# The down projection of an FFN in one streaming-encoder kernel: its transfers in program order by need, its weights and first residuals each in the place of one old pool, its output tiles in a pool of their own

## The chip, the cores and the metric

The kernel runs on one core of a Trainium2 chip. The metric is device time of one execution in microseconds (us): the median of the timed runs. Of 3 runs of the kernel before it was 2545.82 us (2545.22 to 2546.44).

The engines have short names in the profile: PE is TensorE (its weight loads PEld), DVE is VectorE, ACT is ScalarE, POOL is GpSimd, and SP is SyncE, which in this kernel issues nearly all transfers (SPq is its queue).

## The reference

One layer of an encoder: attention with two groups of heads, an output projection, and then a gated FFN whose last product the change concerns.

```python
def trunk_layer(x, pos, chunk, past, lp, rel_bias, lam_init):
    ...
    mix = jnp.concatenate([o_d.reshape(B, L, D_DIFF), o_m.reshape(B, L, D_MLA)], axis=-1)
    x = x + mix @ lp['w_out']
    h = rmsnorm(x, lp['norm_ffn_g'])
    x = x + (jax.nn.silu(h @ lp['ffn_w_gate']) * (h @ lp['ffn_w_up'])) @ lp['ffn_w_down']
    return x, (kd, vd, ckv, krope)
```

The model dimension is 2048, the FFN dimension 5632. There are 576 tokens in all (64 of running streams, 512 new frames). A last RMSNorm with `final_norm_g` follows. Everything is float32.

## The kernel before, in words

Operands are kept transposed, with features on the 128 partitions and the 576 tokens along the free axis, in two halves of 288. A float32 product is made of three matmuls in a faster format: each operand is split into a high part (a rounded copy, made by ScalarE) and a low part (the difference, made by VectorE), and high by high, high weight by low operand, and low weight by high operand are added up. The high and low parts of weights are called `wh` and `wl`, those of the tokens `bh` and `bl`.

The FFN's products go through one level of Winograd's form of Strassen's algorithm (`winograd`): a row of outputs needs seven products, numbered 1 to 7, instead of eight. A weight tile `raw` of 1 MB is loaded; products 1, 2 and 4 split parts of it directly, and the other four first form sums of parts, `ws`: those for products 5 and 7 on GpSimd, for 6 and 3 on VectorE. In the down projection the products come in the order 1, 5, 6, 2, 7, 3, 4 (`CHAIN`), and each has 12 matmuls of 288 columns, eight with `wh` (four operands `bh`, four `bl`) and then four with `wl`. A row has 84. `wh` and `wl` have two buffers each, `raw` has two, `ws` three.

Up and gate projection: 22 steps `u`, in each of which the tile `c` of gate outputs `g` is multiplied into that of the up outputs (GpSimd, `c<-c`, L1312), and the product is stored to HBM (`actspill`), with four sums of it for the later products (`sumspill`).

Down projection: the 22 steps are its contraction, in blocks of 4, 4, 4, 4, 4 and 2. A block has eight rows `d`; row `d` adds to the two residual tiles `y[2d]` and `y[2d+1]`, which are loaded from `x2spill` in the first block and stay in SBUF until the end. For a block, `builder` loads the operands as `bl` (from `actspill` or `sumspill`, 144 KB each), has ScalarE convert each to `bh` and VectorE subtract it. It is a generator: each `next` issues one conversion or one subtraction, and loads run `ahead` operands in front. `blX_S` is the operand of product X in slot S; slots 0 to 3 are used by one block and 4 to 7 by the next. For the first block the builder is advanced by `step` in the seven products of the last up projection, for the others by the products of the block before. The last block has no sums: `plain_rows` takes it in two halves of the tokens, and `finish` transposes the results, scales them on ScalarE or VectorE into output tiles `ot`, and stores them.

What sets the order of the work: TensorE's instructions are always issued as the program writes them. The others go through a scheduler that may move them, unless an instruction is pinned, with `pin` (from the start of the down projection on for the builder's instructions), or an `Engine` object has `ordered` set. In the down projection `pinned[0]` is set. SyncE's transfers are not pinned in the kernel before, so the scheduler puts them in an order of its own.

SBUF is handed out by pools that are stacked from the left (`fr`, `fw`, later `yp`) and from the right (`bc`, `rw`, `fb`, later `yy`). A tile in memory that an older pool held waits until the older tile has been used for the last time. `fb` holds the `c` tiles, `fw` the up projection's `wh`, `wl` and `ws`, `rw` the third buffer of `raw`. The kernel before opens `yy` (all 16 `y`) on the right in the place of `rw` and `fb`, and `yp` on the left in the place of `fw`. `yp` holds `wh`, `wl`, `ws` and also the output tiles `ot` and the small `vc` and `rc`, which is more than `fw` held, so that it reaches into `fb`'s place too.

All engines' operations that go through an `Engine` object carry line 125 in the profile; the matmuls are L1123 (with `wh`) and L1127 (with `wl`), GpSimd's `ws` L1092.

Of the kernel before, what the change touches and what calls it, by code (L numbers as in the profile page):

```python
# [11 lines left out]
F32 = mybir.dt.float32  # L12
# [7 lines left out]
P = 128  # L20
D = 2048
KC = D // P
# [5 lines left out]
TQ = NS + SEQ  # L28
# [103 lines left out]
def encoder_step(  # L132
# [19 lines left out]
    def load(dst, src):  # L152
        Q.dma_start(dst, src)

    def store(dst, src):
        Q.dma_start(dst, src)
# [1068 lines left out]
    def builder(m0, count, plain, ahead, by_product=False):  # L1225
# [21 lines left out]
        for n in range(ahead):  # L1247
            fetch(n)
        for n, (m, p) in enumerate(todo):
            fetch(n + ahead)  # L1250
            hi, lo = operands[m % 8, p]
            pin(S.activation(hi, f32(lo), AF.Copy))
            yield
            pin(V.tensor_tensor(lo, f32(lo), f32(hi), op=ALU.subtract))
            yield
# [16 lines left out]
    blocks = [4, 4, 4, 4, 4, 2]  # L1272

    turn = 0
# [80 lines left out]
    def down_rows(m0, n, d, slots, step):  # L1355
        raws = [load_raw(fr, w_down, m0 * 256, 2 * n, d * 256, 2)]
# [23 lines left out]
    def finish(h, ahead):  # L1380
# [27 lines left out]
        for i, (q, j) in enumerate(groups):  # L1408
            o, n = tok[h][j]
            ps = held.pop(0) if held else turned(q, j)  # L1410
            ot = yp.tile([P, 512], F32, name="ot", tag="ot", bufs=OT_BUFS)
# [9 lines left out]
            yield  # L1421

    pinned[0] = True
    first = 0
    for bi, n in enumerate(blocks):
        slots = [(first + k) % 8 for k in range(n)]
        if bi + 1 < len(blocks):
# [5 lines left out]
            for d in range(KC // 2):  # L1433
                if bi == 0:
                    for i in (2 * d, 2 * d + 1):
                        y.append(yy.tile([P, TQ], F32, name=f"y{i}"))
                        load(y[i], x2spill[i])
# [14 lines left out]
        first += n  # L1452
    close_yp()
    close_fr()
    close_yy()
    close_bc()
# [74 lines left out]
```

## Time and profile before

| | |
|---|---|
| median of 3 runs | 2545.82 us (2545.22 to 2546.44) |
| the profiled execution, its own time | 2543.0 us |
| its span | 2541.2 us |
| busy: PE, PEld | 96%, 94% of the span |
| busy: DVE, ACT, POOL | 71%, 44%, 29% |
| mean DMA | 121 GB/s |
| last matmul of the up projection starts | 1970.28 us |
| first matmul of the down projection starts | 1979.67 us |

Times in the profile are microseconds from the start of the span. A row of the timeline gives the start, the duration, engine, line, operation, output<-input, the number of instructions merged into it, and in brackets how long the engine had been idle before it and what released it. The duration of a merged row runs from its first start to its last end. In the table by windows the busy time of each engine stands with the count of its instructions; PEclk is TensorE's granted clock, 1.00 being full speed. A matmul's own time overlaps with the next one's, so the distance between starts is what counts.

### The profile page before, as it was taken

Reading aid. Unit: us, or ns where it says so; the run is one execution under the profiler, and the core shown is the slowest. Engines: PE = TensorE matmul, PEld = TensorE weight load, DVE = VectorE, ACT = ScalarE, POOL = GpSimd, SP = SyncE. Lnnn points to the kernel's source line nnn. Section 1 sums busy time; section 2 is a strip of 40 time slices with the busy share of each in tenths; the row PEclk is TensorE's granted clock in tenths of the full one; section 3 lists DMA queues with packets and bytes.
Section 4 is the critical chain, followed back from the end, with each engine's and each line's share of the span. In section 5 each row is a group of like instructions: output and inputs, shape, how many; then the busy total and the mean of one; then the engine's idle time right before and its main releaser. Section 6 shows DMA issues by size and latency. Waiting matters only on the chain. (4 is left out here: it accounts for less than half of the span.)

```text
span 2541.2 us, 44865 instructions
## 1 busy us (share of the span) xinstructions
PE 2446.1 (96%) x17847; PEld 2386.6 (94%) x17847; DVE 1799.2 (71%) x2826; ACT 1107.0 (44%) x2008; POOL 739.7 (29%) x614
## 2 busy tenths in 40 slices
PE   7999999989999999999999999999999899999997
PEld 6999999988999888999999999999999799999997
DVE  5555555556555567877777777777777899899975
ACT  5343334334343444444444444444445444444445
POOL 0000000000000164644545445454543222222236
PEclk9999999999999899999999999999999999999999
DMA  7533232334322453333333333333335642452334
GB/s 201 153 86 88 80 85 85 82 97 127 101 89 75 153 155 114 123 133 119 128 99 131 121 123 133 115 120 107 128 128 160 206 156 83 153 161 84 109 102 149
DMA packets 330563, 307.73 MB, mean 121 GB/s; under 512 B 24707, under 2 KB 298506, under 8 KB 330354
## 3 DMA queue, kind: packets, MB, share of 16 engines
q1 hardware_dynamic: 330354, 304.87, 38.3%
q8 instruction: 140, 2.29, 0.4%
q14 instruction: 69, 0.57, 0.1%
HBM read 250.82 MB, written 56.68 MB: 121 GB/s over the span
## 5 line engine op out<-in xcount | busy, mean ns | idle before, releaser
L1123 PE MATMUL m<-bh,wh 128*128 128x288 f32 x3584 | 968.9, 296 | 12.2 <-ACT wh L125 12.2
L1123 PE MATMUL m<-bl,wh 128*128 128x288 f32 x3584 | 968.3, 295 | 0.0
L1123 PEld LDWEIGHTS m<-bh,wh 128*128 128x128 f32 x3584 | 674.3, 188 | 13.2 <-ACT wh L125 13.2
L1123 PEld LDWEIGHTS m<-bl,wh 128*128 128x128 f32 x3584 | 678.1, 189 | 0.1
L1127 PE MATMUL m<-bh,wl 128*128 128x288 f32 x3584 | 585.4, 298 | 17.2 <-DVE wl L125 14.1
L1127 PEld LDWEIGHTS m<-bh,wl 128*128 128x128 f32 x3584 | 512.4, 189 | 30.1 <-DVE wl L125 29.7
L1092 POOL TENSOR_TENSOR ws<-raw 128x512 f32<-128x512 f32 x256 | 343.6, 1350 | 600.1 <-DVE wl L125 344.1
L125 ACT ACTIVATE wh<-ws 128x512 fp32r<-128x512 f32 (+1 forms) x340 | 288.8, 849 | 448.7 <-PE m L1123 293.3
L125 DVE TENSOR_TENSOR wl<-ws,wh 128x512 fp32r<-128x512 f32 (+1 forms) x340 | 379.5, 1116 | 113.7 <-ACT wh L125 113.3
L125 DVE TENSOR_TENSOR wl<-raw,wh 128x512 fp32r<-128x512 f32 x416 | 402.6, 981 | 27.6 <-ACT wh L125 17.4
L125 ACT ACTIVATE wh<-raw 128x512 fp32r<-128x512 f32 x416 | 249.7, 626 | 307.2 <-PE m L1123 274.6
L108 PE MATMUL ps<-xh,wh 128*128 128x296 f32 x960 | 220.8, 311 | 5.2 <-ACT xh L125 3.5
L108 PE MATMUL ps<-xl,wh 128*128 128x296 f32 x960 | 211.0, 301 | 0.9 <-DVE xl L125 0.9
L108 PE MATMUL ps<-xh,wl 128*128 128x296 f32 x960 | 210.8, 301 | 0.2 <-DVE wl L125 0.2
L108 PEld LDWEIGHTS ps<-xh,wh 128*128 128x128 f32 x960 | 157.1, 191 | 9.3 <-ACT xh L125 3.6
L108 PEld LDWEIGHTS ps<-xl,wh 128*128 128x128 f32 x960 | 157.4, 190 | 1.5 <-DVE xl L125 1.5
L108 PEld LDWEIGHTS ps<-xh,wl 128*128 128x128 f32 x960 | 157.2, 190 | 0.9 <-DVE wl L125 0.9
L125 DVE TENSOR_TENSOR y<-y,m 128x288 f32<-128x288 f32 x312 | 139.6, 447 | 25.8 <-PE m L1127 17.6
L125 DVE TENSOR_TENSOR ws<-ws,raw 128x512 f32<-128x512 f32 x128 | 92.3, 722 | 83.9 <-POOL ws L1092 77.5
L125 DVE TENSOR_TENSOR wl<-wr,wh 128x1024 fp32r<-128x1024 f32 (+1 forms) x110 | 117.6, 1070 | 35.3 <-ACT wh L125 33.9
L125 ACT ACTIVATE wh<-wr 128x1024 fp32r<-128x1024 f32 (+1 forms) x110 | 101.6, 928 | 74.1 <-PE ps L108 58.2
L1270 POOL TENSOR_TENSOR c<-c,rb 128x576 f32<-128x576 f32 x44 | 73.0, 1661 | 165.6 <-ACT c L125 165.6
(357 smaller groups left out, 3347.8 us busy)
## 6 DMA issues: line engine op xcount, KB each, us to landing
raw<-in_ffn_w_gate SPq DMA_DIRECT2D x44, 1024.0 KB, 7.0
raw<-in_ffn_w_up SPq DMA_DIRECT2D x44, 1024.0 KB, 5.3
raw<-in_ffn_w_down SPq DMA_DIRECT2D x40, 1024.0 KB, 5.4
wr<-in_w_in SPq DMA_DIRECT2D x60, 512.0 KB, 4.0
actspill<-c SPq DMA_DIRECT2D x44, 288.0 KB, 2.1
sumspill<-c SPq DMA_DIRECT2D x20, 576.0 KB, 3.0
bl<-sumspill SPq DMA_DIRECT2D x80, 144.0 KB, 3.8
bl<-actspill SPq DMA_DIRECT2D x68, 144.0 KB, 3.5
```

Source lines behind the costliest of these rows:

```text
L108: self.tc.keep_in_program_order(self.pe.matmul(out, lhsT, rhs, start=start, stop=stop))
L125: ins = issue(*args, **kwargs)
L1092: engine.tensor_tensor(w[:, k:k + m, :], pick(xs), pick(ys), op=op)
L1123: PE.matmul(banks[p], wh[:, k, :], x, start=first and new and k == 0 and x is hi, stop=False, skip_group_check=not new)
L1127: PE.matmul(banks[p], wl[:, k, :], hi, start=False, stop=last and k == n - 1, skip_group_check=not new)
L1270: G.tensor_tensor(g[:, f, :], g[:, f, :], rb2, op=ALU.mult)
```

## The change

The numerical work stays the same: no operation of the reference's arithmetic is added or dropped. Five things change.

1. SyncE's queue keeps the program's order from the start of the last up projection (`Q.ordered = True`) until the last block. What stands in the program where is then the order of the transfers.
2. The raw tile of `w_down` for a row is fetched two rows ahead (`fetch_raw`), no longer by `down_rows`. The builder of the first block issues its 28 loads product by product, in four at a time, in the first steps of the last up projection; the others' `ahead` stays 4. `y0` to `y3` are loaded before the first row, then two per row.
3. The last two `actspill<-c` stores go to GpSimd's queue. The kernel before has no transfer there.
4. `y0` to `y3` get a pool of their own (`y0`, in `rw`'s place), the rest stay in `yy`; `yp` holds only `wh`, `wl` and `ws` and so fits in `fw`'s place; `ot`, `vc` and `rc` are in a pool `yo` that is opened before the last block.
5. The memset of `vc` is pinned.

```diff
+            if by_product and n % count == count - 1:
+                yield
...
-    start = builder(0, blocks[0], False, 4, True)
+    start = builder(0, blocks[0], False, 2 * blocks[0], True)
...
                     done[0] += 1
+                    if done[0] == 1:
+                        Q.ordered = True
+                        fetch_raw(0, blocks[0], 0)
+                    if done[0] < 3:
+                        next(start)
...
+    fetch_raw(0, blocks[0], 1)
     for f in range(2):
-        store(actspill[FC - 2 + f], out["u"][:, f, :])
+        G.dma_start(actspill[FC - 2 + f], out["u"][:, f, :])
     close_fb()
     close_rw()
+
+    y0, close_y0 = pool("y0", "right")
...
-        raws = [load_raw(fr, w_down, m0 * 256, 2 * n, d * 256, 2)]
+        raws = [fetched.pop((m0, d))]
...
-        vc = yp.tile([P, 3], F32, name=f"vc{h}")
-        rc = yp.tile([P, 3], F32, name=f"rc{h}")
-        V.memset(vc, 1.0)
+        vc = yo.tile([P, 3], F32, name=f"vc{h}")
+        rc = yo.tile([P, 3], F32, name=f"rc{h}")
+        pin(V.memset(vc, 1.0))
...
-            ot = yp.tile([P, 512], F32, name="ot", tag="ot", bufs=OT_BUFS)
+            ot = yo.tile([P, 512], F32, name="ot", tag="ot", bufs=OT_BUFS)
...
+                if bi == 0 and d == 0:
+                    for i in range(4):
+                        accumulator(i)
+                if bi == 0 and 2 * d + 4 < KC:
+                    for i in (2 * d + 4, 2 * d + 5):
+                        accumulator(i)
                 down_rows(first, n, d, slots, step)
+                if d + 2 < KC // 2:
+                    fetch_raw(first, n, d + 2)
+                elif bi + 2 < len(blocks):
+                    fetch_raw(first + n, blocks[bi + 1], d + 2 - KC // 2)
...
+            Q.ordered = False
+            yo, close_yo = pool("yo")
```

What this does to the order on the engines, at the transition from the up to the down projection. (Names with a number at the end are tiles; `c_21275` is the last up tile, `m` a bank of PSUM.) ScalarE, before, from the last operand of product 3 on:

```order
L125 ACTIVATE bh3_3_21607<-bl3_3_21608 128x288
L125 ACTIVATE c_21275<-m_21276 128x288
L125 ACTIVATE bh4_0_21614<-bl4_0_21615 128x288
L125 ACTIVATE bh4_1_21619<-bl4_1_21620 128x288
L125 ACTIVATE bh4_2_21624<-bl4_2_21625 128x288
L125 ACTIVATE bh4_3_21629<-bl4_3_21630 128x288
L125 ACTIVATE wh_21660<-raw_21657 128x512
L125 ACTIVATE bh1_4_21677<-bl1_4_21678 128x288
L125 ACTIVATE wh_21696<-ws_21694 128x512
L125 ACTIVATE wh_21716<-ws_21714 128x512
```

ScalarE, in the changed kernel, from the same operand on:

```order
L125 ACTIVATE bh3_3_21570<-bl3_3_21571 128x288
L125 ACTIVATE bh4_0_21606<-bl4_0_21607 128x288
L125 ACTIVATE bh4_1_21611<-bl4_1_21612 128x288
L125 ACTIVATE c_21275<-m_21276 128x288
L125 ACTIVATE bh4_2_21616<-bl4_2_21617 128x288
L125 ACTIVATE wh_21673<-raw_21308 128x512
L125 ACTIVATE bh4_3_21621<-bl4_3_21622 128x288
L125 ACTIVATE wh_21709<-ws_21707 128x512
L125 ACTIVATE wh_21729<-ws_21727 128x512
L125 ACTIVATE wh_21751<-raw_21308 128x512
L125 ACTIVATE wh_21771<-ws_21769 128x512
L125 ACTIVATE wh_21794<-ws_21792 128x512
```

The copy `c<-m` moved behind the second operand of product 4, the first `wh` stands between the third and the fourth, and block 1's first operands (`bh1_4`, `bh2_4`), which stood between the first weights, follow behind the seventh weight, below these rows.

GpSimd, before, from the gate's last scaling (`rb2`) on; `c<-c` is the product of gate and up:

```order
L1270 TENSOR_TENSOR c_21038<-c_21038,rb2_9503 128x576 x2
L1312 TENSOR_TENSOR c_21275<-c_21275,c_21038 128x576 x2
L1092 TENSOR_TENSOR ws_21694<-raw_21657 128x512
L1092 TENSOR_TENSOR ws_21756<-raw_21657 128x512
L1092 TENSOR_TENSOR ws_21846<-raw_21824 128x512
```

GpSimd, in the changed kernel, at the same place:

```order
L1271 TENSOR_TENSOR c_21038<-c_21038,rb2_9503 128x576 x2
L1323 TENSOR_TENSOR c_21275<-c_21275,c_21038 128x576
L1338 DMA actspill_69<-c_21275 128x576
L1091 TENSOR_TENSOR ws_21707<-raw_21308 128x512
L1323 TENSOR_TENSOR c_21275<-c_21275,c_21038 128x576
L1091 TENSOR_TENSOR ws_21769<-raw_21308 128x512
L1338 DMA actspill_69<-c_21275 128x576
L1091 TENSOR_TENSOR ws_21859<-raw_21644 128x512
```

The two halves of `c<-c` are apart now, with a store and the first row's first `ws` between them, and the second store stands behind the second `ws`.

SyncE, before, from the last operand of product 3 on:

```order
L125 DMA bl3_3_21608<-actspill_69 128x288
L125 DMA bl3_4_21734<-actspill_69 128x288
L125 DMA raw_21824<-in_ffn_w_down 128x8x256
L125 DMA bl4_0_21615<-sumspill_70 128x288
L125 DMA bl4_1_21620<-sumspill_70 128x288
L125 DMA bl4_2_21625<-sumspill_70 128x288
L125 DMA bl4_3_21630<-sumspill_70 128x288
L125 DMA actspill_69<-c_21275 128x576 x2
L125 DMA bl4_4_21684<-sumspill_70 128x288
L125 DMA bl4_5_21908<-sumspill_70 128x288
L125 DMA bl3_5_22041<-actspill_69 128x288
L125 DMA bl2_6_22173<-actspill_69 128x288
```

SyncE, in the changed kernel, from the first operand of product 4, which here stands directly behind `bl3_3`:

```order
L125 DMA bl4_0_21607<-sumspill_70 128x288
L125 DMA bl4_1_21612<-sumspill_70 128x288
L125 DMA bl4_2_21617<-sumspill_70 128x288
L125 DMA bl4_3_21622<-sumspill_70 128x288
L125 DMA raw_21644<-in_ffn_w_down 128x8x256
L125 DMA y0_21660<-x2spill_68 128x576
L125 DMA y1_21662<-x2spill_68 128x576
L125 DMA y2_21664<-x2spill_68 128x576
L125 DMA y3_21666<-x2spill_68 128x576
L125 DMA y4_21668<-x2spill_68 128x576
L125 DMA y5_21670<-x2spill_68 128x576
L125 DMA bl1_4_21691<-actspill_69 128x288
```

Ahead of product 4 there is no `raw` and no operand of a later block (`bl3_4`) any more. The second `raw`, then `y0` to `y5`, then block 1's operands follow, and the stores are gone from this queue. At the start of each later block the `raw` of its second row now precedes all operands that are built for the block after; in the kernel before 17 of these stood ahead of it in block 1, for instance.

More of the change, by code (lines that the diff above doesn't have):

```diff
@@ L150, in encoder_step, with transfer @@
     S.preload_act_table_set("natural_log_exp_and_others")
-    def load(dst, src):
+    def transfer(dst, src):
         Q.dma_start(dst, src)
-    def store(dst, src):
-        Q.dma_start(dst, src)
+    load = store = transfer
     def const(name, shape, src):
@@ L1272, in encoder_step, with fetch_raw @@
     blocks = [4, 4, 4, 4, 4, 2]
+    fetched = {}
+    def fetch_raw(m0, n, d):
+        fetched[m0, d] = load_raw(fr, w_down, m0 * 256, 2 * n, d * 256, 2)
     turn = 0
     norm = token_norm()
-    start = builder(0, blocks[0], False, 4, True)
+    start = builder(0, blocks[0], False, 2 * blocks[0], True)
     for u in range(FC // 2):
@@ L1421, in finish, with accumulator @@
             yield
+    def accumulator(i):
+        y.append((y0 if i < 4 else yy).tile([P, TQ], F32, name=f"y{i}"))
+        load(y[i], x2spill[i])
     pinned[0] = True
@@ L1433, in encoder_step @@
             for d in range(KC // 2):
[L1434 to L1437, printed above, removed]
+                if bi == 0 and d == 0:
[4 more added lines that the diff above has]
+                        accumulator(i)
                 down_rows(first, n, d, slots, step)
+                if d + 2 < KC // 2:
+                    fetch_raw(first, n, d + 2)
+                elif bi + 2 < len(blocks):
+                    fetch_raw(first + n, blocks[bi + 1], d + 2 - KC // 2)
             for _ in build:
@@ L1452, in encoder_step @@
         first += n
+    close_yo()
     close_yp()
@@ L1455, in encoder_step @@
     close_yy()
+    close_y0()
     close_bc()
```

## The prediction

> **What bounds the kernel now.** I begin with the page's busy times, since they say which engine sets the pace.
>
> ```profile
> PE 2446.1 (96%) x17847; PEld 2386.6 (94%) x17847; DVE 1799.2 (71%) x2826; ACT 1107.0 (44%) x2008; POOL 739.7 (29%) x614
> ```
>
> TensorE is busy for 96%, so only its idle time, its half clock and its spacing can move the end. Next come TensorE's waits from the end of the up projections on (columns: total us, times, longest).
>
> ```profile
> PE m L1127 <- DVE wl L125: 11.7, 23, 1.0
> PE m L1123 <- ACT wh L125: 9.6, 2, 9.1
> ```
>
> One wait of 9.1 us stands out; the 23 on `wl` are half a microsecond each. The table by stage says where they lie (columns: window, its length, busy time and count of PE, PEld, DVE, ACT, POOL, then TensorE's granted clock, DMA share, GB/s).
>
> ```profile
> 1950.00:1970.30 20.30, 20.30 (x155) 20.30 (x153) 19.29 (x36) 15.48 (x35) 2.45 (x3) 1.00 0.91 271
> 1970.30:1975.86 5.56, 0.27 (x3) 0.04 (x1) 3.37 (x3) 0.72 (x2) 3.06 (x2) 1.00 1.01 329
> 1975.86:1986.10 10.24, 5.46 (x21) 5.12 (x22) 6.37 (x12) 4.11 (x9) 3.18 (x3) 0.50 0.85 267
> 1986.10:1994.45 8.35, 8.35 (x65) 8.35 (x64) 7.41 (x14) 4.03 (x8) 1.90 (x2) 1.00 0.60 224
> 2000.00:2400.00 400.00, 385.97 (x2813) 374.61 (x2811) 371.18 (x651) 186.18 (x348) 89.39 (x68) 1.00 0.40 127
> ```
>
> The hole lies between the up and the down projection, with the transfer engines full (1.01), and 10.24 us of half clock follow it. In the 400 us of steady rows TensorE is busy for 386 and VectorE for 371, 93%: a row has little cover on either. What holds the hole, engine by engine:
>
> ```profile
> 1979.67 0.61 PE L1123 MATMUL m<-bh,wh 128*128 128x288 f32 x1 [9.10 <-ACT wh L125]
> 1982.93 1.33 PE L1127 MATMUL m<-bh,wl 128*128 128x288 f32 x4 [0.97 <-DVE wl L125]
> ```
>
> ```profile
> 1970.61 0.41 ACT L125 ACTIVATE c<-m 128x288 f32<-128x288 f32 x1
> 1976.24 1.54 ACT L125 ACTIVATE bh<-bl 128x288 fp32r<-128x288 f32 x4 [5.22 <-DMA bl<-sumspill]
> 1978.99 0.63 ACT L125 ACTIVATE wh<-raw 128x512 fp32r<-128x512 f32 x1 [1.20 <-DMA actspill<-c]
> ```
>
> ```profile
> 1965.21 2.29 SPq L125 DMA_DIRECT2D bl<-actspill  x5
> 1967.60 0.38 SPq L125 DMA_DIRECT2D raw<-in_ffn_w_down  x1
> 1968.07 4.05 SPq L125 DMA_DIRECT2D bl<-sumspill  x4
> 1972.22 1.49 SPq L125 DMA_DIRECT2D actspill<-c  x2
> ```
>
> ScalarE waits 5.22 us for product 4's `bl` tiles, which SyncE issued behind a 1 MB `raw` of the next row, then 1.20 us for the two stores whose old memory the first `wh` overwrites. Everything around the span is 2543.0 - 2541.2 = 1.8 us, and this execution lies 2.8 us under the median of 2545.82; I sum against it and add the 2.8 at the end.
>
> **The change, part by part.**
>
> *Loads in the order of need, and the weights out of the stores' memory.* `bl4` no longer stands behind the `raw`, nor behind loads for block 1. SyncE is then where it now issues the `raw`, 1967.60, when it issues `bl4`. The nearest landings are those of these loads from 1944 to 1964 (the last column is the median):
>
> ```profile
> bl<-sumspill SPq DMA_DIRECT2D x17, 144.0 KB, 3.7
> bl<-actspill SPq DMA_DIRECT2D x13, 144.0 KB, 2.8
> ```
>
> I take 2.3, a little under the lower one, since now 17 fewer loads stand in the queue: `bl4_0` at 1969.9, two `bh` of 0.4, `c<-m` of 0.41 at 1970.6, a third `bh`, then the first `wh`, 0.63, done near 1972.0. The stores no longer stand before it. So TensorE starts at 1972.0 instead of 1979.67. With 3.7 it would start at 1973.4, and the sum would not change, since what follows ends later.
>
> *The stores on GpSimd.* Eight matmuls later it needs the first `wl`, and here the order on POOL decides: a product `c<-c`, a store, `ws`, the other `c<-c`, `ws`, where before both `c<-c` came first and the stores were SyncE's.
>
> ```profile
> 1970.30 3.06 POOL L1312 TENSOR_TENSOR c<-c 128x576 f32<-128x576 f32 x2 [15.31 <-issue]
> 1979.21 2.51 POOL L1092 TENSOR_TENSOR ws<-raw 128x512 f32<-128x512 f32 x2 [5.86 <-DMA bl<-sumspill]
> ```
>
> ```profile
> 1969.34 0.46 DVE L125 TENSOR_TENSOR bl<-bl,bh 128x288 fp32r<-128x288 f32 x1 [1.01 <-ACT bh L125]
> 1969.72 0.45 DVE L125 TENSOR_TENSOR c<-c,m 128x288 f32<-128x288 f32 x1
> 1970.08 3.59 DVE L125 TENSOR_TENSOR bl<-bl,bh 128x288 fp32r<-128x288 f32 x3
> 1980.52 1.75 DVE L125 TENSOR_TENSOR ws<-ws,raw 128x512 f32<-128x512 f32 x1 [1.39 <-POOL ws L1092]
> 1982.19 0.68 DVE L125 TENSOR_TENSOR wl<-raw,wh 128x512 fp32r<-128x512 f32 x1
> ```
>
> ```profile
> L125 DVE TENSOR_TENSOR ws<-ws,raw 128x512 f32<-128x512 f32 x128 | 92.3, 722 | 83.9 <-POOL ws L1092 77.5
> ...
> actspill<-c SPq DMA_DIRECT2D x44, 288.0 KB, 2.1
> ```
>
> These rows show an exclusion: three `bl` of 0.46 took 3.59, until POOL's `c<-c` were over, and the `ws` on VectorE took 1.75 beside POOL's second `ws`, where its mean on the page is 0.72. VectorE's operation ends some 0.55 behind POOL's (1982.27 against 1981.72). Now the sum. The add `c<-c,m` stands behind a `bl` that waited 1.01; with its load earlier I let POOL's first `c<-c` start at 1969.3 and end at 1970.75 (half of 3.06, less rounding). Then the store's issue on POOL, which no row shows. Its lower bound is SyncE's 0.38 for an issue, its upper what the landing of such a store takes, 2.1 on the page (`actspill<-c`), or 5 if POOL is held out by VectorE as VectorE is held out here. I take 1.0, nearer to the row of an issue. `ws` starts at 1971.8. From there: `ws` 1.29, POOL's other `c<-c` 1.44 (it follows at once and keeps VectorE out, as POOL's second `ws` does at 1980.52), VectorE's `ws` 0.55 behind it, POOL's second `ws` 1.16, `bl4_2` 0.36, `wl` 0.60: 5.4 us, so `wl` at 1977.2.
>
> Now TensorE: it starts at 1972.0, stops at 1973.1, and waits to 1977.2, against 1982.93 before. That is 5.7 us earlier with the same eight matmuls done. But the idle pieces are 1.4 and 4.1 us. The clock fell 5.3 us after the last up matmul, at 1975.86, and came back 3.2 us after 1982.93; I expect it halved again behind the 4.1 us, for 3 to 6 us after 1977.2. At full clock 155 matmuls start in 20.30 us, 0.131 each or 1.6 for a product's twelve, and at half clock half of the time is lost: 1.6 before, 1.5 to 3.0 after, -0.6 at the middle. The next products' `wl` are late too, while POOL and VectorE catch up, 0.5 to 1.0 each for two of them: -1.3. Gain at row 1: 5.7 - 0.6 - 1.3 = **3.8 us**.
>
> The Trainium skill, "SBUF — State Buffer", the box on the "DVE blocks DMA" trap under "SBUF: two separate sides", speaks against the store's new queue: descriptors of a GpSimd DMA are written by GpSimd itself, which VectorE locks out while it works in a two-port mode, and one such transfer grew from about 620 to 3100 ns. No row of before shows a GpSimd DMA; with 2.5 us more for the first store the sum would keep 1.3 of the 3.8.
>
> *Raw tiles two rows ahead, then the next block's operands.* At a block's first row SyncE now issues the `raw` of its second row, and only then the operands built for the block after, where before up to 17 of them stood ahead of it. The trace of before has one place where such operands follow a `raw`, in the row that starts block 2:
>
> ```profile
> 2172.01 0.38 SPq L125 DMA_DIRECT2D raw<-in_ffn_w_down  x1
> 2172.48 1.83 SPq L125 DMA_DIRECT2D bl<-sumspill  x3
> ```
>
> ```profile
> 2175.49 0.63 ACT L125 ACTIVATE wh<-raw 128x512 fp32r<-128x512 f32 x1 [0.63 <-PE m L1123]
> ...
> 2180.30 0.45 ACT L125 ACTIVATE bh<-bl 128x288 fp32r<-128x288 f32 x1 [2.53 <-DMA bl<-sumspill]
> ```
>
> ```profile
> 2181.31 0.40 PE L1123 MATMUL m<-bh,wh 128*128 128x288 f32 x1 [0.55 <-ACT wh L125]
> 2183.43 0.80 PE L1127 MATMUL m<-bh,wl 128*128 128x288 f32 x4 [0.81 <-DVE wl L125]
> ```
>
> A `bl` issued behind the 1 MB landed 7.8 us later, ScalarE waited 2.53, TensorE lost 0.55 + 0.81 = 1.36. In the change the first such conversion stands right behind the row's fourth `wh`, the one at 2175.49 here, so ScalarE is there at 2176.1, 4.1 us behind the `raw`'s issue.
>
> ```profile
> raw<-in_ffn_w_down SPq DMA_DIRECT2D x40, 1024.0 KB, 5.4
> ```
>
> A landing at 5.4, this `raw`'s own median, leaves a wait of 1.3, which the weights one product ahead (1.6) nearly hide. I put 0.4 at each of four boundaries, bounds 0 and 1.36: **-1.6**; the 1.36 lost at 2181 goes, since those conversions now come earlier, in the order of need: +1.4.
>
> *Output tiles in their own pool.* The last block's buffers are opened later, and its first transposes stand earlier. The waits there, and an eviction's durations (min/median/max ns):
>
> ```profile
> 2502.47 0.40 PE L205 MATMUL m<-bh,wh 128*128 128x288 f32 x1 [1.44 <-ACT wh L125]
> ```
>
> ```profile
> 2518.84 0.63 ACT L125 ACTIVATE wh<-raw 128x512 fp32r<-128x512 f32 x1 [1.06 <-DMA raw<-in_ffn_w_down]
> ```
>
> ```profile
> L125 DVE TENSOR_SCALAR ot<-m,rc x12: 729/740/752, 2503.9 to 2537.1; 128x512 f32<-128x512 f32 x6, 64x512 f32<-64x512 f32 x2, 96x512 f32<-96x512 f32 x2, 32x512 f32<-32x512 f32 x2
> ```
>
> Two output evictions of 0.74 now stand before one `wl`, and a `raw` behind four output stores, where ScalarE already waits 1.06 for one: -0.8, bounds -2.5 (the two evictions and another 1.06) and +0.5 (the third of the 1.44 that a buffer freed sooner could save).
>
> Sum: 3.8 - 1.6 + 1.4 - 0.8 = 2.8 us. 2543.0 - 2.8 + 2.8 = **2543.0**.
>
> **The rivals.**
>
> *The hole closes whole.* If VectorE's `ws` gets in before POOL's other `c<-c`, and the store's issue is 0.4, `wl` comes near 1974.2 (`ws` 1971.15 to 1972.45, VectorE's 0.72, `bl4_2` and `wl` alone): the idle pieces are 1.4 and 1.1, the clock stays, and row 1 gains 8.7 + 1.6 - 1.3 = 9.0. With -1.0 elsewhere that is 8.0: 2537.8. For it speaks that the 5.22 and 1.20 us go whole; against it POOL's second `ws`, which kept VectorE out at 1980.52. 0.22.
>
> *Each boundary pays (slower).* The mechanism is the `bl` that lands behind the `raw` at the four boundaries. It decides once a landing takes over 4.1 + 1.6 = 5.7 us; at the 7.8 of 2172 ScalarE waits 3.7, TensorE 2.1 in each of four, 8.4 in all, less the 1.4 that before had. With -0.8 in the tail and a first store of 3 us (gain 1.8 at row 1) the change loses 6.0: 2551.8; with the full 3.8 it loses 4.0: 2549.8. For it: that one row. Against it: transfers run at a share of 0.40 in these rows, and ScalarE's waits for such a load come to 3.5 us in the whole of 2000 to 2500:
>
> ```profile
> ACT bh L125 <- DMA bl<-sumspill: 3.5, 2, 2.5
> ```
>
> 0.14.
>
> *GpSimd's stores hold the line.* `y4` on SyncE waits for both, and behind it stand `y5`, the five operands of block 1 and the third `raw`. The first of these is converted behind the seventh `wh` of the first row, which in before is this one:
>
> ```profile
> 1991.01 0.63 ACT L125 ACTIVATE wh<-raw 128x512 fp32r<-128x512 f32 x1 [0.96 <-PE m L1123]
> ```
>
> 3.8 earlier and 0.6 behind its start, that is 1987.8. With 2.8 to land and 0.95 for two issues, the second store must have landed by 1984.0; my sum has it issued at 1976.8 and landed at 1978.9. If it lands 14 us later, at 1993, ScalarE is 9 us late and TensorE, 1.6 ahead, loses 7.4: 2551.0. 0.06. The rule of the Trainium skill above works in this direction, and no run here shows it yet.
>
> *It doesn't do what it says:* `bl4` lands as late as before because the operand memory comes free late or the transfers are full (0.91 in 1950 to 1970). From a landing of 1975.5 on, `wh` again is last, and the gain at row 1 is 1 or less, which the -1.0 elsewhere takes: 2545.8. 0.10.
>
> **How the numbers follow.** My forecast has 0.48, with its own range 2540 to 2546. A measurement of this kernel can tell about 0.2% from no change, 5.1 us. Faster by more: 0.20 of the whole closing and 0.04 of the forecast, 0.24. Slower by more: 0.08 of the boundaries, 0.06 of the stores, 0.14. The rest, 0.62, is within. Range: down to 2537.0, which takes in most of the closed hole, and up to 2550.5, which takes in the boundaries at the full gain; it leaves out some 0.17.
>
> **What would show it.** The first down matmul near 1972, the eight behind it, then a wait of about 4 us on `wl`; `ws` on POOL at 1971.8; a shorter half-clock window, no `DMA` releaser on the first `wh`; row 1 four us earlier; a `raw` ahead of `bl` at each boundary with ScalarE waiting 1 to 2 us. Wrong would be: the first `wl` before 1975 (I overrated POOL), or TensorE waiting for `wh` at rows 8, 16, 24, 32 by over 1 us (I underrated the boundaries).

## The result and the profile after

The changed kernel takes 2549.78 us (median of 12 runs, 2547.42 to 2553.96), the kernel before 2545.58 in the same measurement (12 runs, 2539.82 to 2549.86). The ratio is **1.0018, with a 95% interval of 1.0010 to 1.0025**: 4.2 us slower, where 2543.0, a little faster than before, was forecast. (The forecast's range went up to 2550.5, to take in its rival of the boundaries; its direction was wrong.)

Single runs of one kernel lie up to 10 us apart, and profiled executions differ too: the last up matmul ends at 1970.57 us in the profile of before and at 1975.42 in that of after. That difference arises earlier still: the last 200 weight conversions ahead of that point take the same 451.3 us in every profile. So every stretch below is counted from the end of the last up matmul ("+"). From there to the end of the span it is 570.6 us before and 575.3 after, 4.7 more, which agrees with the ratio.

TensorE's waits in the down projection of the changed kernel (total us, times, longest; the lines are L1122 and L1126 now):

```profile
PE m L1126 <- DVE wl L125: 16.9, 26, 5.3
PE m L204 <- ACT wh L125: 4.6, 3, 2.8
...
PE m L1122 <- DVE y L125: 3.0, 4, 1.2
...
PE m L1122 <- ACT wh L125: 1.5, 1, 1.5
```

The 9.1 us on `wh` have become 1.5. In its place stands one wait of 5.3 on `wl` (0.97 before); and two kinds are new, four waits on `y` and one of 2.8 us in the last block. The windows around the transition (columns as in the table of before):

```profile
1975.42:1980.53 5.11, 1.32 (x8) 1.09 (x8) 3.07 (x3) 2.50 (x6) 4.78 (x4) 1.00 0.98 288
1980.53:1987.36 6.83, 3.86 (x16) 3.86 (x16) 5.18 (x7) 1.21 (x2) 2.90 (x4) 0.50 0.60 220
1987.36:2000.00 12.64, 12.30 (x89) 11.74 (x88) 10.41 (x21) 6.23 (x14) 1.97 (x2) 1.00 0.58 183
```

The clock still halves, for 6.83 us instead of 10.24, and 3.86 of these lie behind the first `wl`-matmul (3.2 before). TensorE and ScalarE there:

```profile
1976.90 0.40 PE L1122 MATMUL m<-bh,wh 128*128 128x288 f32 x1 [1.48 <-ACT wh L125]
1983.50 1.33 PE L1126 MATMUL m<-bh,wl 128*128 128x288 f32 x4 [5.28 <-DVE wl L125]
```

```profile
1974.73 0.96 ACT L125 ACTIVATE bh<-bl 128x288 fp32r<-128x288 f32 x2 [1.01 <-DMA bl<-sumspill]
1975.60 0.39 ACT L125 ACTIVATE c<-m 128x288 f32<-128x288 f32 x1
1975.89 0.43 ACT L125 ACTIVATE bh<-bl 128x288 fp32r<-128x288 f32 x1
1976.23 0.62 ACT L125 ACTIVATE wh<-raw 128x512 fp32r<-128x512 f32 x1
```

No transfer releases the first `wh` any more. GpSimd and VectorE, which make the first `wl` late:

```profile
1974.42 2.61 POOL L1323 TENSOR_TENSOR c<-c 128x576 f32<-128x576 f32 x1 [14.20 <-issue]
1977.34 0.71 POOL L1338 DMA_DIRECT2D actspill<-c  x1 [0.31 <-POOL c L1323]
1978.07 1.27 POOL L1091 TENSOR_TENSOR ws<-raw 128x512 f32<-128x512 f32 x1
1979.29 1.41 POOL L1323 TENSOR_TENSOR c<-c 128x576 f32<-128x576 f32 x1
1980.65 1.26 POOL L1091 TENSOR_TENSOR ws<-raw 128x512 f32<-128x512 f32 x1
1981.86 0.58 POOL L1338 DMA_DIRECT2D actspill<-c  x1
```

```profile
1974.21 3.13 DVE L125 TENSOR_TENSOR bl<-bl,bh 128x288 fp32r<-128x288 f32 x5
1979.38 3.09 DVE L125 TENSOR_TENSOR ws<-ws,raw 128x512 f32<-128x512 f32 x1 [2.04 <-POOL ws L1091]
1982.40 0.45 DVE L125 TENSOR_TENSOR bl<-bl,bh 128x288 fp32r<-128x288 f32 x1
1982.77 0.68 DVE L125 TENSOR_TENSOR wl<-raw,wh 128x512 fp32r<-128x512 f32 x1
```

VectorE's `ws` takes 3.09 us, where its mean on the page of before is 0.72: it ends 0.56 after GpSimd's second `ws`, so it waited for the `c<-c` and for that `ws` too. And GpSimd's first `c<-c` takes 2.61, beside five `bl` of VectorE. The first row of block 1, on SyncE, ScalarE, VectorE and TensorE:

```profile
2079.43 0.38 SPq L125 DMA_DIRECT2D raw<-in_ffn_w_down  x1
2079.90 1.01 SPq L125 DMA_DIRECT2D bl<-actspill  x2
```

```profile
2082.89 0.63 ACT L125 ACTIVATE wh<-raw 128x512 fp32r<-128x512 f32 x1 [0.96 <-PE m L1122]
2085.21 0.82 ACT L125 ACTIVATE bh<-bl 128x288 fp32r<-128x288 f32 x2 [1.68 <-DMA bl<-actspill]
```

```profile
2085.68 0.88 DVE L125 TENSOR_TENSOR bl<-bl,bh 128x288 fp32r<-128x288 f32 x1 [1.19 <-ACT bh L125]
2086.49 0.44 DVE L125 TENSOR_TENSOR y<-y,m 128x288 f32<-128x288 f32 x1
```

```profile
2087.07 0.37 PE L1122 MATMUL m<-bh,wh 128*128 128x288 f32 x1 [0.49 <-DVE y L125]
```

ScalarE waits 1.68 us for the operand behind the `raw`, VectorE 1.19 us for ScalarE before it can subtract, and behind the subtraction in VectorE's queue stands the `y` addition whose bank TensorE wants. And the last block, ScalarE, SyncE, TensorE:

```profile
2510.61 3.30 SPq L125 DMA_DIRECT2D out<-ot  x4
2514.01 0.54 SPq L125 DMA_DIRECT2D raw<-in_ffn_w_down  x1
```

```profile
2520.00 0.63 ACT L125 ACTIVATE wh<-raw 128x512 fp32r<-128x512 f32 x1 [2.73 <-DMA raw<-in_ffn_w_down]
```

```profile
2520.69 0.40 PE L204 MATMUL m<-bh,wh 128*128 128x288 f32 x1 [2.75 <-ACT wh L125]
```

**The account.** I take the starts of ScalarE's weight conversions, seven to a row, as the start of a row, and cut the stretch into five pieces: from the last up matmul to row 1, rows 1 and 2, the four boundary rows (8, 16, 24 and 32), the other rows up to the last block, and from there to the end of the span. For all kernels with a timed comparison (ratio to the kernel before; 5 runs of e2, 11 or 12 of the others):

| kernel | to row 1 | rows 1, 2 | boundary rows | other rows | last block | sum | ratio (95%) |
|---|---|---|---|---|---|---|---|
| before | 22.0 | 22.8 | 49.6 | 390.1 | 86.1 | 570.6 | |
| **after** | 18.5 | 24.1 | 51.7 | 391.8 | 89.2 | 575.3 | 1.0018 (1.0010-1.0025) |
| e1 stores on SyncE | 19.6 | 22.7 | 52.4 | 393.1 | 87.7 | 575.5 | 1.0023 (1.0014-1.0032) |
| e2 last block in order | 18.1 | 24.0 | 52.1 | 393.7 | 91.2 | 579.1 | 1.0032 (1.0020-1.0044) |
| e3 operands before raw | 17.8 | 24.1 | 48.6 | 392.3 | 88.5 | 571.3 | 1.0008 (0.9999-1.0017) |
| e4 order free | 17.4 | 23.0 | 49.4 | 391.6 | 89.5 | 570.9 | 0.9999 (0.9991-1.0008) |
| e5 = e4, raw in pairs | 17.7 | 23.5 | 48.8 | 391.2 | 85.8 | 566.9 | 0.9987 (0.9978-0.9996) |
| e6 = e4, ot with weights | 23.7 | 22.9 | 49.7 | 389.4 | 86.3 | 572.0 | 1.0004 (0.9995-1.0013) |
| e7 order, old pools | 21.3 | 23.0 | 51.7 | 391.5 | 87.8 | 575.2 | 1.0013 (1.0004-1.0022) |
| e9 = e3, raw in pairs | 18.1 | 24.0 | 48.5 | 392.7 | 85.4 | 568.8 | 0.9986 (0.9977-0.9995) |
| e10 = e5, stores on SyncE | 17.3 | 23.5 | 50.4 | 390.4 | 85.3 | 566.9 | 0.9981 (0.9972-0.9989) |
| e11 before, new pools | 17.4 | 22.9 | 51.1 | 390.8 | 88.0 | 570.1 | 0.9995 (0.9986-1.0004) |

Each row of numbers is one profiled execution. The change gains 3.5 up to row 1 and loses 1.3, 2.1, 1.7 and 3.1 behind it. In the boundary rows the pinned kernels whose operands stand behind the `raw` take 51.7 to 52.4 (after, e1, e2, e7), and each of the four rows pays. Where the order is free it is 48.8 to 51.1 (before, e4, e5, e6, e10, e11): TensorE pays for a late operand in one or two of the four, not in the same ones each time.

### The profile page after: what moved, and what is told of

It is laid out like the page before. It is cut to its first block, busy times and chain, and to the rows that moved or that the text cites. A ratio compares the mean times of both kernels' runs of the same rounds, so it can differ in the third digit from the quotient of the medians.

```text
span 2550.7 us, 44822 instructions
## 1 busy us (share of the span) xinstructions
PE 2452.8 (96%) x17847; PEld 2391.2 (94%) x17847; DVE 1800.3 (71%) x2826; ACT 1106.4 (43%) x2008; POOL 740.3 (29%) x616
## 5 line engine op out<-in xcount | busy, mean ns | idle before, releaser
L1122 PE MATMUL m<-bh,wh 128*128 128x288 f32 x3584 | 968.7, 296 | 7.1 <-ACT wh L125 4.1
L1122 PE MATMUL m<-bl,wh 128*128 128x288 f32 x3584 | 967.4, 295 | 0.0
L1122 PEld LDWEIGHTS m<-bh,wh 128*128 128x128 f32 x3584 | 673.9, 188 | 9.0 <-ACT wh L125 4.8
L1122 PEld LDWEIGHTS m<-bl,wh 128*128 128x128 f32 x3584 | 677.4, 189 | 0.1
L1126 PE MATMUL m<-bh,wl 128*128 128x288 f32 x3584 | 586.6, 299 | 22.1 <-DVE wl L125 19.3
L1126 PEld LDWEIGHTS m<-bh,wl 128*128 128x128 f32 x3584 | 512.5, 189 | 36.0 <-DVE wl L125 34.9
```

The costliest lines, as they stand in the source:

```text
L1122: PE.matmul(banks[p], wh[:, k, :], x, start=first and new and k == 0 and x is hi, stop=False, skip_group_check=not new)
L1126: PE.matmul(banks[p], wl[:, k, :], hi, start=False, stop=last and k == n - 1, skip_group_check=not new)
```

## The experiments

My theory after the result: the gain is there as forecast, and the order of the transfers gives it back in three places (boundaries, some rows, last block). The rival: VectorE, at 93% of the steady rows, takes back any lead, and the new waits only show where.

**e1, the stores on SyncE.**

```diff
-        G.dma_start(actspill[FC - 2 + f], out["u"][:, f, :])
+        store(actspill[FC - 2 + f], out["u"][:, f, :])
```

> The changed kernel with one line undone: the last two stores go to SyncE again, behind the second raw and before y0. All stretches are counted from the end of the last up matmul: in the profile of the changed kernel the first wl-matmul comes at +8.1 us, before at +12.4, and the span ends at +575.3, before at +570.6. Theory (the stores cost little; what is late on the first wl is GpSimd's other c<-c and the exclusion): the first wl at +7 to +8, y4 on SyncE issued some us earlier, the end within 1 us of +575.3, ratio to the kernel before 1.001 to 1.002. Rival (the GpSimd stores, and y4 behind them, cost the first rows): row 2 starts 2 us or more earlier than in the changed kernel, the end at +573 or less.

Measured: the first `wl` at +6.4, the end at +575.5, ratio 1.0023. GpSimd's stores are not what makes the change slow. With them away the first `wl` is 1.7 us earlier and rows 1 and 2 are as before, but row 0 loses more, so that row 3 starts at +42.3, against +42.6 in the changed kernel: in the pinned queue the stores now stand ahead of `y0`, and TensorE waits for an addition to `y` that the kernel with GpSimd's stores didn't wait for.

```profile
1978.54 1.33 PE L1126 MATMUL m<-bh,wl 128*128 128x288 f32 x4 [3.67 <-DVE wl L125]
1986.62 0.41 PE L1122 MATMUL m<-bh,wh 128*128 128x288 f32 x1 [1.34 <-DVE y L125]
```

**e2, the last block in program order, its raw tiles two rows ahead.**

```diff
-            Q.ordered = False
+            plain = [load_raw(fr, w_down, first * 256, 2 * n, d * 256, 2) for d in range(2)]
...
-                    plain_rows(first, n, d, (h,), slots, squares)
+                    plain_rows(first, n, d, (h,), slots, squares, plain.pop(0))
+                    if h * 8 + d + 2 < 16:
+                        plain.append(load_raw(fr, w_down, first * 256, 2 * n, (d + 2) % 8 * 256, 2))
```

> The changed kernel with the last block's raw tiles fetched two rows ahead and SyncE kept in program order to the end, so that no raw stands behind four output stores. From the start of the last block's first weights to the end of the span the profile shows 90.8 us in the changed kernel and 87.7 before. Theory (the fourteenth raw stands behind four output stores, ScalarE waits 2.73 for it, TensorE loses 2.90): that stretch falls back by 2.5 to 3.5 us to some 87.7, no wait of ScalarE for a raw above 1 us; the rows before it don't change; the ratio to the kernel before falls from 1.0018 to about 1.0006. Rival (the output tiles' new place or the earlier transposes cost it): the stretch stays within 1 us of 90.8.

A miss: the last block got longer, 91.2 against 89.2. (The 90.8 and 87.7 above start one weight conversion, 1.6 us, ahead of the table's 89.2 and 86.1.) The edit doesn't do what I wrote it for. Even two rows ahead, a load still stands behind the first output store in the program; the store can't go before its tile has been scaled, and the queue holds the load back with it.

```profile
PE m L204 <- ACT wh L125: 5.6, 3, 3.5
```

The wait is the same kind as before the edit, moved forward by one load; the longest is 3.5 us, and behind it TensorE's clock halves for 3.41 us, which it doesn't there in the changed kernel. The run left theory and rival open.

**e3, the next block's first two operands ahead of the raw.**

```diff
+                if d == KC // 2 - 1 and bi + 2 < len(blocks):
+                    nx = first + n + blocks[bi + 1]
+                    primed = builder(nx, blocks[bi + 2], bi + 3 == len(blocks), 4, prime=2)
+                    next(primed)
                 if d + 2 < KC // 2:
                     fetch_raw(first, n, d + 2)
```

> The changed kernel with the first two operand loads of the block after next issued ahead of the last raw that a block fetches, at three of the four boundaries and at the fourth in the plain form. In the changed kernel the weight conversion in rows 8, 16, 24 and 32 that follows these operands comes 1.4, 1.5, 2.2 and 1.5 us late. Theory (the operand lands late because it is issued behind 1 MB): these delays fall under 0.5 us each, the four waits of TensorE on y (3.0 us in all) go, the rows from 1 to 40 get 2 to 4 us shorter, ratio 1.0006. Rival (VectorE sets the pace, and a row's loss is made up or taken anyway): the delays go, but rows 1 to 40 stay within 1 us.

Measured: the boundary rows 48.6 instead of 51.7, rows 1 to 40 2.7 us shorter, ratio 1.0008. TensorE's waits in the rows of blocks 0 to 4:

```profile
PE m L1126 <- DVE wl L125: 12.8, 24, 1.1
```

The four waits on `y` are gone. The theory holds for the boundaries, and in this profile a wait taken away there does come through to the end: VectorE's pace doesn't swallow it. By the timed runs alone e3 and the changed kernel aren't quite apart (0.9999 to 1.0017 against 1.0010 to 1.0025); e9 below has the same edit.

**e4, the order left to the scheduler.**

```diff
-                        Q.ordered = True
```

> The changed kernel without the pinned order of SyncE's queue: pools, two-rows-ahead fetches and GpSimd stores stay, the scheduler places the transfers, and a raw stands before product 4's operands again. Theory (the order of transfers gives the earlier first wh, and takes it back in the later rows): the first wh-matmul waits 5 us or more again, rows 8 to 40 run as before, without the boundary waits, the end at +573 to +576. Rival (the new places of the pools alone free the first wh, the order matters little): the first wh-matmul stays within 2.5 us of the last up matmul.

Here the rival to my expectation held. The `raw` stands before product 4's operands again, and yet:

```profile
1974.00 0.40 PE L1122 MATMUL m<-bh,wh 128*128 128x288 f32 x1 [1.41 <-ACT wh L125]
1979.15 1.33 PE L1126 MATMUL m<-bh,wl 128*128 128x288 f32 x4 [3.82 <-DVE wl L125]
```

The scheduler has put the first `wh` ahead of product 4's four `bh`, and product 4 is the last of the row; the `wh` no longer waits for the stores (with the old place of the output tiles, in e6, it stands behind the four `bh` and waits again). So the order of the loads has no share in the gain. The boundary rows are 49.4 and the end is at +570.9. The last block still takes 89.5: TensorE waits 1.7 us there behind a `raw`, and behind that wait the clock halves for 3.41 us.

**e5, the same with the last block's raw tiles in pairs of rows.**

```diff
+    def load_pair(m0, n, k):
+        r = fr.tile([P, 2 * n, 512], F32, name="raw", tag="raw", bufs=2)
...
-            Q.ordered = False
+            Q.ordered = True
+            pairs = [load_pair(first, n, k) for k in range(2)]
```

> The changed kernel with SyncE's order free until the last block (as in the fourth run, which ends at +570.9 from the last up matmul, 89.5 of them from the last block's first weights on), and in the last block pinned, with the raw tiles in eight loads of two rows each, two loads ahead, so that none has to wait behind the first output stores. In the second run the raw of row 12 stood behind the first output store and TensorE lost 3.59 there; in the changed kernel it is 2.90, in the fourth run 1.87. Theory (a raw behind output stores is the tail's loss): no wait for wh above 0.5 us after the table loads, the last stretch 86 to 87.5, the end at +567.5 to +569, ratio to the kernel before 0.9985 to 0.9995. Rival (the place of the output tiles, not the raw, makes the tail longer): the stretch stays at 89 or more.

Measured: the last block 85.8, ratio 0.9987, the interval below 1. Of the waits above 1 us only the one behind ScalarE's table load and the one on `ot` are left; these stand in before too, whose two rows come second:

```profile
PE m L1408 <- ACT ot L125: 2.5, 1, 2.5
PE m L204 <- ACT wh L125: 1.4, 1, 1.4
...
PE m L1391 <- ACT ot L125: 2.5, 1, 2.5
PE m L205 <- ACT wh L125: 2.0, 2, 1.4
```

The halved clock of e4's last block is gone with the wait. So a raw tile queued behind output stores was the last block's loss, with what the wait did to the clock in e4, and e2 had only moved it.

**e6, output tiles back in the weights' pool, order free.** The edit replaces `yo` by `yp` in the three tiles' lines and unpins the memset.

> The fourth run's kernel (SyncE's order free) with the output tiles, vc and rc back in the weights' pool and the memset unpinned, as before the change; y0 to y3 stay apart. Theory (the weights' pool that reaches into the last c tiles' memory is what held the first wh): the first wh waits for the stores again, now issued by GpSimd with the second landing some 13 us after the last up matmul, so the first wh-matmul comes at +10 to +14 and row 1 starts no earlier than before (+22 to +25); the tail goes back to 86 to 87.5. Rival (the order of ScalarE's work, weights before product 4's operands, gave the gain): the first wh-matmul at +1.5 to +3.

Measured: first `wh`-matmul at +10.1, row 1 at +23.7, last block 86.3.

```profile
1977.05 0.63 ACT L125 ACTIVATE wh<-raw 128x512 fp32r<-128x512 f32 x1 [3.87 <-DMA actspill<-c]
```

The stores hold the first weights again, 3.87 us of it, and the last block is as short as before the change. The place of the output tiles is a trade: 6.3 us at the transition (23.7 against 17.4) for 3.2 in the last block (89.5 against 86.3).

**e7, the pinned order with the old pools.** In the changed kernel the pools `y0` and `yo` are undone.

> The changed kernel's order (SyncE pinned, raw two rows ahead, stores on GpSimd) with the old pools: y in one pool, output tiles in the weights' pool. Theory (pools free the first wh; the pinned order costs at the boundaries and in rows 1 and 2, 3 to 4 us in all): the first wh-matmul at +10 or later, the boundary rows 8, 16, 24 and 32 as long as in the changed kernel (51.7 us together, 49.6 before), the end at +578 or more, ratio 1.003 or more. Rival (order and pools give back each other's loss): ratio 1.001 or less.

The mechanism as expected, the size not: the stores landed earlier than I took them to, the first `wh`-matmul comes at +7.6, and the ratio is 1.0013, between theory and rival. The boundary rows are 51.7, as in the changed kernel; with the order free they were 49.7 (e6) and 49.4 (e4), and up to 51.1 in e11 below.

**e8, one of GpSimd's products left out.** The second half of the last gate-times-up product isn't made; its store carries the up tile alone. It has one profiled execution and no timed comparison.

```diff
-            G.tensor_tensor(w[:, f, :], w[:, f, :], g[:, f, :], op=ALU.mult)
+            if u < FC // 2 - 1 or f == 0:
+                G.tensor_tensor(w[:, f, :], w[:, f, :], g[:, f, :], op=ALU.mult)
```

> The fourth run's kernel with one multiplication left out: the second half of the last gate-times-up product is not made, so its store carries the up tile alone; this takes GpSimd's other c<-c (1.41 us) out from between its two ws. In the fourth run the first wl-matmul comes at +6.56. Theory (that c<-c keeps VectorE's ws and with it the first wl back): the first wl-matmul at +3.5 to +4.8, the half-clock window gone or shorter than 3.5 us, row 1 starts 2 to 4 us earlier than the +17.4 of the fourth run. Rival (the first wl waits for GpSimd's ws and store, not for the c<-c): the first wl-matmul at +6 or later.

A miss: the first `wl` at +6.7, not at +4.

```profile
1976.19 1.27 POOL L1091 TENSOR_TENSOR ws<-raw 128x512 f32<-128x512 f32 x1
1977.39 0.56 POOL L1338 DMA_DIRECT2D actspill<-c  x1
1977.97 1.27 POOL L1091 TENSOR_TENSOR ws<-raw 128x512 f32<-128x512 f32 x1
```

```profile
1977.50 2.31 DVE L125 TENSOR_TENSOR ws<-ws,raw 128x512 f32<-128x512 f32 x1 [1.66 <-POOL ws L1091]
```

The store took the product's place, and VectorE's `ws`, which starts at 1977.50 with nothing but the store's issue on GpSimd, still ended only 0.57 behind the second `ws`. Part of the miss is a different start: the first `ws` begins at +2.5 here, against +1.5 in e4, because the product before it also begins 1.0 later. Counted from that `ws`, the first `wl` comes 4.3 us later, against 5.1 in e4, so leaving the product out saved 0.8 of its 1.41. Whether the store's issue itself kept VectorE out isn't shown: the second `ws` began 0.47 us after VectorE's start, before an add of 0.72 could be over, and in the changed kernel VectorE's `ws` ran to its end (1982.47) beside GpSimd's issue of the second store (1981.86 to 1982.44).

**e9, the pinned order with both mends (e3 and the pairs of e5).**

> The changed kernel, SyncE pinned as it is, with two mends: the operands ahead of the raw at the boundaries (third run) and the last block's raw tiles in pairs (fifth run). Theory (the losses of the boundaries and of the tail are two separate ones that add up): from the changed kernel's end at +575.3 from the last up matmul come off 2.7 (rows 1 to 40 of the third run) and 3.4 (the last stretch of the fifth), so the end at +568 to +570.5, ratio to the kernel before 0.9985 to 1.0000. Rival (they share a cause, VectorE's pace): the end at +572 or later.

Measured: +568.8, ratio 0.9986 (0.9977 to 0.9995). The two losses add up, which the rival excludes. Rows 1 and 2 stay at 24.0 and the other rows at 392.7.

**e10, e5 with the stores on SyncE.** The edit of e1 on e5.

> The fifth run's kernel with the two stores on SyncE instead of GpSimd, SyncE's order free before the last block. In the fifth run the first wl-matmul comes at +7.3 from the last up matmul, row 1 starts at +17.7, the end is at +566.9. Theory (the store on GpSimd delays its ws by 0.71 and 0.58 us, and y4 waits for it; nothing else): the first wl at +5.5 to +6.8, row 1 0.5 to 1.5 us earlier, the end at +565.5 to +567, ratio 0.998 to 0.9995. Rival (on SyncE the stores hold up the loads behind them): row 1 starts at +18.5 or later, the end at +568 or later.

Measured: first `wl` at +6.4, row 1 at +17.3, the end at +566.9, ratio 0.9981 (0.9972 to 0.9989), the lowest of all, though not apart from e5 and e9 by their intervals. Moving the stores to GpSimd brings nothing that the pools don't, and at the first `wl` it costs something. Without them VectorE's `ws` gets in between GpSimd's product and its second `ws`:

```profile
1973.20 1.39 POOL L1322 TENSOR_TENSOR c<-c 128x576 f32<-128x576 f32 x1
1974.55 1.71 POOL L1091 TENSOR_TENSOR ws<-raw 128x512 f32<-128x512 f32 x1
```

```profile
1973.27 1.87 DVE L125 TENSOR_TENSOR ws<-ws,raw 128x512 f32<-128x512 f32 x1 [2.53 <-POOL ws L1091]
```

It ends 0.55 behind the product here, and so it does in e1 and e11 (1.89 us), the other kernels with the new pools and the stores on SyncE. In the changed kernel and in e2 to e5 and e9, with the stores on GpSimd, it started just as it does here, beside the product, and ended 0.56 behind the second `ws`, after 3.09 to 3.10 us. That goes with the place of the stores in all nine kernels; why it does, no run shows.

**e11, the kernel before with the new pools alone.**

> The kernel before with the change of the pools alone: y0 to y3 apart, weights alone in fw's place, output tiles, vc and rc in a pool of their own, the memset pinned; transfers, fetches and the stores on SyncE as before. Theory (the pools bring the whole gain at the transition and, by the later raw, the tail's loss): the first wh-matmul at +1.3 to +2.5, row 1 at +17 to +18.5 (before +22.0), rows 1 to 40 within 1.5 us of the kernel before, the last stretch 88.5 to 90 (before 86.1), the end at +569 to +571.5, ratio 0.999 to 1.001. Rival (the gain needs the order of the loads too): the first wh-matmul at +4 or later.

Measured: row 1 at +17.4, last block 88.0, ratio 0.9995. TensorE's start:

```profile
1977.29 0.61 PE L1123 MATMUL m<-bh,wh 128*128 128x288 f32 x1 [3.59 <-ACT wh L125]
1980.18 1.33 PE L1127 MATMUL m<-bh,wl 128*128 128x288 f32 x4 [0.60 <-DVE wl L125]
```

The first `wh` comes at +3.59, later than the theory had it and not as late as the rival, and it doesn't matter: the `wl` behind it comes at +6.5 as in e4, and row 1 at the same time. Of the transition's gain the pools bring all. The rest of the theory missed: rows 1 to 40 are by the table 2.3 us longer than before, most of it in boundary rows of 51.1, in which two of the four wait for a late operand with SyncE's order as free as before. And the last block's 88.0 isn't the later `raw`. TensorE waits no longer for `wh` there than before (1.8 us in two against 2.0 in two), but behind ScalarE's table load its clock halves for 3.41 us, where in the kernel before it stays at 1.00:

```profile
2504.91:2508.32 3.41, 3.41 (x17) 3.23 (x16) 2.33 (x4) 1.38 (x3) 1.13 (x2) 0.50 0.40 117
```

## Why the prediction was wrong

I forecast 2.8 us won and measured 4.7 lost in the profiles. Of these 7.5 the transition has 0.3, the boundaries 1.9, the last block 2.3, and the rows between, which I had put at nothing, 3.0.

**The transition: right in sum, in part by luck.** I forecast 3.8 us at row 1 and measured 3.5. The first `wh` came where I had it. From GpSimd's first `ws` to the first `wl` I had 5.4; it is 1983.50 - 1978.07 = 5.43, though in another order: I let VectorE's `ws` in ahead of GpSimd's second one, and it came behind it. `ws` itself starts 2.65 us after the last up matmul instead of my 1.2, since the exclusion works the other way round too: GpSimd's `c<-c` took 2.61 beside VectorE's `bl`, where I had 1.44. The first `wl` is so 1.5 us later than forecast; that the losses behind it were 0.8 instead of my 1.9 and made up for most of it was luck. The credit I gave was wrong, though: I put the earlier start on the order of the loads and the pools together, and e4 and e11 show that the pools alone bring the gain at row 1 (17.4 in both). My rival "it doesn't do what it says" had seen that the loads could be late, but not that it wouldn't matter.

**The boundaries: the step that failed first.** I put 0.4 on each of four and then gave back 1.4 for the one place where before had such a wait: -0.2 in all. Measured is -2.1: the four rows take 12.6 to 13.4 us, where a row of before without such a wait has 11.9 to 12.0, so each costs 0.7 to 1.4. ScalarE's waits for these operands come to 7.7 us in four in the changed kernel:

```profile
ACT bh L125 <- DMA bl<-actspill: 7.7, 4, 2.5
```

That is 1.9 each, against the 1.3 that I had worked out and thought covered by weights one product ahead. The cover was misjudged, and e3, with the operands ahead of the `raw`, gives the loss back: what TensorE waited for was not the next `wh` but a bank, whose addition to `y` stood in VectorE's queue behind the late operand. I named neither that queue nor who waits behind it.

**The last block: mis-sized.** The mechanism, a `raw` behind four output stores, was in the prediction with -0.8, and a bound of -2.5; it cost 3.1. I had sized it by the one wait of 1.06 for a `raw` that before shows, and two evictions; ScalarE then waited 2.73 in one piece, and TensorE as long. With the raw out of the stores' way, e5 has 3.4 and e9 3.8 less there than the changed kernel.

**The rows between: left out, and the cause stays open.** I had nothing for rows 1 and 2 beyond the transition, nor for the other rows, and gave no reason; they cost 1.3 and 1.7. Rows 1 and 2 take 24.0 to 24.1 in after, e2, e3 and e9, which have the pinned order, GpSimd's stores and the new pools together, 23.5 in e5 and e10, and 22.7 to 23.0 in the others. Taking GpSimd's stores out of the changed kernel (e1) brings them to 22.7, but row 0 loses nearly as much there, so the loss may be one of the transition that comes later; it wasn't tried apart. The rest is seen but not settled either: the other rows take 391.5 to 393.7 us where SyncE is pinned and 389.4 to 391.6 where it isn't, and `bl` transfers took 4.9 to 5.0 us to land instead of 3.5 to 3.8 (medians of the two pages), being issued behind a `raw`. No run took that apart, and single executions differ by about 2 us there.

**The rivals.** "Each boundary pays" named 2549.8, and 2549.78 was measured, but by another sum: it had the boundaries cost 7.0 us more than before, where they cost 2.1. That the number was met is luck. Against "GpSimd's stores hold the line" stand e1 and e10: they didn't make the change slow. The Trainium skill's rule ("SBUF — State Buffer", "SBUF: two separate sides") that VectorE can lock GpSimd out of writing a transfer's descriptors is not shown by any run here. The two stores landed 5.6 us after their issue, at the median, against 2.1 on SyncE in the rest of the kernel, but six loads of the same size that SyncE issued in the same 15 us took 5.8; and the issue itself took only 0.71 and 0.58 us, so the 2.5 us worked out from the page did not fall on the path.

```profile
y<-x2spill SPq DMA_DIRECT2D x6, 288.0 KB, 5.8
actspill<-c POOLq DMA_DIRECT2D x2, 288.0 KB, 5.6
```

## What to carry to other kernels

A queue in program order is only as good as the place of every line in it: a large load or a store that runs late holds back all that is written behind it, so look for what the next waits behind, also in the queue of the engine that consumes it. When a wait is removed at one place, sum the losses elsewhere as carefully as the gain: here 3.5 us were won and 8.2 lost in four places of which two had been named, and undervalued. And test the parts alone: the pools by themselves brought all of the gain at the transition, the pinned order cost time at the boundaries and, mended (e9), was no faster than a free one (e5), and the stores on GpSimd brought nothing.

## What the runs showed of the hardware

The exclusion between GpSimd and VectorE goes both ways: GpSimd's `c<-c` took 2.61 us beside VectorE's `bl` and 1.41 where it had begun before VectorE's `ws`, and VectorE's `ws` took 3.09 beside two GpSimd operations, where its mean on the page of before is 0.72. How many operations VectorE waits for differed with the queue of the stores: in the three kernels with the new pools and SyncE's stores (e1, e10, e11) its `ws` got in behind one, and GpSimd's second `ws` then took 1.71 to 1.73; in the six with stores on GpSimd and the product between the two `ws` (after, e2 to e5, e9) it waited for both, and the second `ws` took 1.25 to 1.27. The reason isn't shown.

The half clock came in pieces of 3.41 us: 10.24 (three) behind a first idle time of 9.1, and 6.83 (two) behind idle times of 1.48 and 5.28 with eight matmuls between them. Its length does not follow from the idle time alone: e9 has idle times of 2.01 and 3.21 at the same place, and 10.24 us of half clock. It began there 2.1 us after the last up matmul, against 5.3 in the kernel before and 5.1 in the changed one.
